# RWKV-7 scan: separate loads for r/k and v, a third buffer for the inverse's blocks, and a merge ordered behind the running sequence's first step

## The chip, the cores and the metric

The kernel runs on one core of a Trainium2 chip. The metric is the device time of one execution in microseconds (us); lower is better. A core has a matrix engine (TensorE, PE in the profile, with its weight loads as PEld), a vector engine (DVE), a scalar engine (ACT), a general engine (GpSimd, POOL) and a queue engine (SyncE, SP) which here issues nearly all the DMAs. Every engine works through its own queue in order. Engines wait for each other by semaphores.

## The reference

A decoder trunk of two layers, batch 1, 1024 tokens, width 1024. Layer 0 mixes tokens by multi-head latent attention, layer 1 by RWKV-7 time mixing; both add four heads of attention over 256 memory tokens, an output projection, a post-LayerNorm and a squared-ReLU MLP of width 4096. The change touches only the RWKV-7 mixer of layer 1, which has 12 heads of 64:

```python
p_tm = p_tm + (_token_shift(p_tm) - p_tm) * mu
r, k, v, hw, ha, hg = split(p_tm)
decay = exp(-exp(-softplus(-(w0 + tanh(hw) @ w2)) - 0.5))
a = sigmoid(a0 + ha @ a2);  g = sigmoid(hg) @ g2
kk = k * k_k / ||k * k_k||              # per head
k = k * (1 + (a - 1) * k_a)
# for every token t, per head, S is 64 x 64:
sa = S @ (-kk_t)
S = S * decay_t + sa (kk_t * a_t)^T + v_t k_t^T
y_t = S @ r_t
# group norm of y, plus (r . k . r_k) v, times g, then the output projection
```

## The kernel before, in words

The sequential recurrence is computed in chunks of 64 tokens (CH). One unit of work is two pairs of heads (u = 0, 1) times 256 tokens (QT), that is four chunks; three groups of pairs times four quarters of the sequence make 12 units, n = 0 to 11. Within a chunk the recurrence needs the inverse of a unit triangular 64 x 64 matrix per head. It is found in two stages: the 16 x 16 blocks on the diagonal by substitution on POOL, and then two merges (masks M1 and M2) that join them to blocks of 32 and 64 on PE and DVE.

A unit goes through these functions of `rwkv`:

- `prepare(n)` (L946 on) loads r, k and v in one tile `rkv` (L958) and the decay and a inputs in `sga` (L961), and finds the norm of k: squares on ACT (L967), sums on PE (L970), inverse square root on DVE, transposes and spreading on PE (L976, L982), `kk` on DVE (L986).
- `early(n)` calls `decays` for u = 0, 1 (decay products, the tiles AR, F, BK; F reads k on L1058, AR reads r on L1059, `rkk` reads r on L1069; the products of BK and AR on L1066, masked into `NR` on L1067) and then `substitute(n)`: NR is written to DRAM (L1082), the diagonal blocks read back with another layout (L1084), solved on POOL (L1085 to L1091), written to DRAM (L1093).
- `late(n)` makes what the sequence needs: masked products into `ark` (L1012, L1016), transposes `bkt` (L1020 on), `bv` (L1026, L1027, reads v) and the transposed v into `W` (L1031, reads v).
- `merge(n)` loads the solved blocks into `X` (L1101, two buffers) and does the two merges: transpose on DVE (L1106), products (L1110), mask (L1112), products (L1116), sum into X (L1117).
- `sequence(n)` is the recurrence over the four chunks. A step is: products with the state W (L1142), copy `Rs` (L1152), products with X (L1164), copy into W (L1168), products with bkt (L1172), scaled into the next W (L1175).
- `finish(n)` is the group norm and the gate, and stores o (L1208).

Iteration n of the loop writes down `sequence(n)`, `merge(n + 1)`, `prepare(n + 2)`, `early(n + 2)`, `finish(n)`, `late(n + 2)` and then `FILL[n]` pieces of other work. These pieces, 88 in all, come from one generator: 40 half projections of the layer's input (24 matmuls each, for r, k, v and the memory queries), 16 pieces of memory attention and 32 pieces of the output projection's first half (6 matmuls each). Twelve are done before the scan, `FILL[12]` at its start. Each batch of pieces is spread over the four steps of `sequence(n)` by `issue_after(anchor)`.

No queue order is written out by hand. A planner walks the program with estimated costs and puts on each engine, from what is ready in its own timeline, what was written down first. `issue_after(ins)` adds an edge: instructions of the block on the engine of `ins` are queued behind `ins`. Tiles are ring buffers of `bufs` slots; a new tile waits until all readers of the slot's last tile are done. The tiles of `ld` (rkv and sga) have two slots, which is one unit; NR has three, X two, AR, BK and rkk two (one unit).

After the loop come the rest of the pieces (`fill(99)`), the load of the output weights for o's rows 6 and 7, and the fetch of rows 4 and 5 of o. Then `out_and_ff` loads two more parts of w_out (L1816, through the raw buffers) and does the second half of the output projection.

Of the kernel before, what the change touches and what calls it, by code (L numbers as in the profile page):

```python
# [10 lines left out]
F32 = mybir.dt.float32  # L11
# [9 lines left out]
P = 128  # L21
# [5 lines left out]
NFF = 4096 // P  # L27
NM = 256
CH = 64
FILL = (4, 3, 4, 3, 4, 3, 11, 9, 7, 7, 7, 7, 7)  # L30
QT = 256
ALPHA = 4.0 ** 0.25
DECAY_C = math.exp(-0.5)
# [33 lines left out]
class Trunk:  # L67
# [588 lines left out]
    def rwkv(self, rows_src):  # L656
        nc, a, sm = self.nc, self.a, self.sm
        res_src = rows_src
        NC = QT // CH
# [5 lines left out]
        with ExitStack() as so:  # L665
# [131 lines left out]

            pieces = project()

            anchors = []  # L800

            def fill(n):
                for _ in range(n):
# [102 lines left out]
            with ExitStack() as s:  # L906
# [39 lines left out]
                def prepare(n):  # L946
                    d = DU[n] = {}
                    gr, q = n // 4, n % 4
                    d["gs"] = gs = slice(q * QT, (q + 1) * QT)
                    d["pa"] = pa = 2 * gr  # L950
                    d["ark"] = ARK[n % 2]
                    d["NR"] = up.tile([P, 2, NC, 2 * CH], F32, name="NR", bufs=3)
                    d["pC"] = up.tile([P, 2, NC], F32, name="pC", bufs=3)
                    d["AR"], d["BK"], d["rkk"] = [], [], []
                    ld, sa = [], []
                    for u in range(2):
                        t = lp.tile([P, 3, QT], F32, name="rkv")
                        nc.sync.dma_start(t, rkv_d[pa + u].rearrange("(j i) t -> i j t", i=P)[:, :, gs])  # L958
                        ld.append(t)
                        t = lp.tile([P, 2, QT], F32, name="sga")  # L960
                        nc.sync.dma_start(t, lo_d[pa + u].rearrange("(j i) t -> i j t", i=P)[:, 0:2, gs])  # L961
                        sa.append(t)

                    pk = psx.tile([P, 8], F32, name="ps_ss", tag="x")
                    for u in range(2):
                        sq = t1("sq")
                        nc.scalar.activation(sq, ld[u][:, 1, :], AF.Square, scale=self.col("kk", pa + u))  # L967
                        for t in range(2):
                            c = 4 * u + 2 * t
                            nc.tensor.matmul(pk[:, c : c + 2], sq[:, t * P : (t + 1) * P], hsel, start=True, stop=True)  # L970
                    ss = sm.tile([P, 8], F32, name="ss")
                    nc.vector.tensor_scalar(ss, pk, 1e-24, None, op0=ALU.max)
                    rs = self.rsqrt(ss, 8, "kk")
                    nc.vector.tensor_copy(cmp_[:, 0:8], rs)
                    pT = psx.tile([P, P], F32, name="ps_kT", tag="x")
                    nc.tensor.transpose(pT, cmp_, self.ident)  # L976
                    cT = tp.tile([P, P], F32, name="kT")
                    nc.scalar.copy(cT, pT)
                    pb = psx.tile([P, 2, QT], F32, name="ps_kb", tag="x")
                    for u in range(2):  # L980
                        for t in range(2):
                            nc.tensor.matmul(pb[:, u, t * P : (t + 1) * P], selk[:, 2 * u + t, :], cT, start=True, stop=True)  # L982
                    d["kk"] = []
                    for u in range(2):
                        kk = t1("kk", 2)
                        nc.vector.scalar_tensor_tensor(kk, ld[u][:, 1, :], self.col("kk", pa + u), pb[:, u, :], op0=ALU.mult, op1=ALU.mult)  # L986
                        d["kk"].append(kk)
                    d["ld"], d["sa"] = ld, sa
# [8 lines left out]

                def late(n):
                    d = DU[n]
                    ld = d["ld"]  # L1000
                    d["bv"] = up.tile([P, 2, QT], F32, name="bv")
                    d["bkt"] = up.tile([P, 2, NC, P], F32, name="bkt")
                    d["W"] = W = up.tile([P, 2, NC, 2, CH], F32, name="W")
                    if n % 4 == 0:
                        nc.gpsimd.memset(W[A, :, 0, 0, :], 0.0)
                        nc.gpsimd.memset(W[B, :, 0, 1, :], 0.0)
                    for u in range(2):
                        ark, AR, BK = d["ark"][:, u], d["AR"][u], d["BK"][u]
                        ga = psg.tile([P, NC, P], F32, name="ps_ga", tag="g")
                        for c in range(NC):  # L1010
                            for R, hd in HD:
                                nc.tensor.matmul(ga[HD[1 - hd][0], c, :], BK[R, c, 1, :], AR[R, c, :, :].rearrange("p h t -> p (h t)"), start=True, stop=True)  # L1012
                        for R, hd in HD:
                            O = HD[1 - hd][0]
                            nc.scalar.copy(ark[R, :, hd, :], AR[R].rearrange("p c h t -> p c (h t)"))
                            nc.vector.tensor_mul(ark[O, :, hd, :], ga[O], MM[O, None, :].broadcast_to([64, NC, P]))  # L1016

                        pbk = psg.tile([P, NC, P], F32, name="ps_bk", tag="g")
                        for c in range(NC):
                            nc.tensor.transpose(pbk[:, c, :], BK[:, c, :, :].rearrange("p h t -> p (h t)"), self.ident)  # L1020
                        nc.scalar.copy(d["bkt"][:, u, :, 0:64], pbk[:, :, 0:64])
                        for R, hd in HD:
                            nc.scalar.copy(d["bkt"][R, u, :, 64:P], pbk[HD[1 - hd][0], :, 64:P])

                        pbv = psx.tile([P, QT], F32, name="ps_bv", tag="x")
                        nc.tensor.matmul(pbv, blk, d["rkk"][u], start=True, stop=True)  # L1026
                        nc.vector.tensor_mul(d["bv"][:, u, :], pbv, ld[u][:, 2, :])  # L1027
                    pv = psg.tile([P, 2, 2, P], F32, name="ps_vt", tag="g")
                    for u in range(2):
                        for t in range(2):  # L1030
                            nc.tensor.transpose(pv[:, u, t, :], ld[u][:, 2, t * P : (t + 1) * P], self.ident)  # L1031
                    ev = W.rearrange("p u (w two) h i -> p u w two h i", two=2)
                    for e, R in ((0, A), (1, B)):
                        nc.scalar.copy(ev[B, :, :, e, 0, :], pv[R, :, :, 0:64])
                        nc.scalar.copy(ev[A, :, :, e, 1, :], pv[R, :, :, 64:P])
# [40 lines left out]
                def substitute(n):  # L1076
# [14 lines left out]
                    nc.gpsimd.memset(xb.rearrange("p s t -> p (s t)")[:, 0:256:17], 1.0)  # L1091
                    for h in range(8):
                        nc.sync.dma_start(blocks_of(xd, h), xb[8 * h : 8 * h + 8])  # L1093

                def merge(n):
                    d = DU[n]
                    xd = XD[n % 2]
                    N = d["NR"][:, :, :, 0:CH]
                    d["X"] = X = up.tile([P, 2, NC, CH], F32, name="X")
                    for R, hd in HD:  # L1100
                        nc.sync.dma_start(X[R].rearrange("p u c t -> p (u c t)"), rows_of(xd, hd))  # L1101
                    f2 = lambda t: t.rearrange("p c t -> p (c t)")
                    for M in (M1, M2):
                        for u in range(2):
                            XT = up.tile([P, NC, CH], F32, name="XT", bufs=1)
                            nc.vector.transpose(f2(XT), f2(X[:, u]))  # L1106
                            pq = psi.tile([P, NC, CH], F32, name="ps_q", tag="i")
                            for c in range(NC):
                                for R, hd in HD:
# [10 lines left out]
                def sequence(n):  # L1120
# [13 lines left out]
                                mm(yq[R, u, c, :], Rm[R, u, c, :], W[R, u, c, hd, :], start=False, stop=True, skip_group_check=True)  # L1134

                    anchors.clear()
                    for c in range(NC):
                        more = c < NC - 1 or nW is not None
                        qt = psq.tile([P, 2, 3, CH], F32, name="ps_q", tag="q")
# [9 lines left out]
                                    for R, hd in HD:  # L1149
                                        mm(qt[R, u, 2, :], self.ident[:, 64 * hd : 64 * hd + 64], W[:, u, c, hd, :], start=False, stop=False, skip_group_check=True)  # L1150
                        Rs = up.tile([P, 2, CH], F32, name="Rs", bufs=1)
                        nc.vector.tensor_copy(Rs, qt[:, :, 0, :])  # L1152
                        with ExitStack() as order:
                            for ins in first:
                                order.enter_context(self.tc.issue_after(ins))
# [63 lines left out]
                for n in range(N):  # L1219
                    sequence(n)  # L1220
                    if n + 1 < N:
                        merge(n + 1)
                    if n + 2 < N:
                        prepare(n + 2)
                        early(n + 2)
                    finish(n)
                    if n + 2 < N:
                        late(n + 2)
                    for c, m in enumerate(anchors):
                        with self.tc.issue_after(m):  # L1230
                            fill((FILL[n] + c) // NC)
                fill(99)
                self.wo = [self.load_split(a["w_out"][1, k * P : (k + 1) * P, :], (1024,)) for k in (6, 7)]
                for kt in (4, 5):
                    self.fetch_o(kt, kt - 2, slice(0, QT * 3))


    def out_part(self, psm, R, tt, nh, ks, wo, first):
# [684 lines left out]
```

## Time and profile before

| | |
|---|---|
| median of 3 runs | 2718.97 us (2716.73 to 2728.4) |
| profiled execution | 2722.41 us, span 2720.6 us |
| PE busy / weight loads | 2552.2 us (94%) / 2064.3 us (76%) |
| DVE busy | 1795.9 us (66%) |
| ACT busy | 1194.1 us (44%) |
| POOL busy | 212.1 us (8%) |
| mean granted PE clock | 0.965 |
| scan, 1397 to 2014 us | 617.0 us: PE busy 527.26, DVE 403.32, clock 0.90 |

The span is that of the profiled execution; its own time is a little longer, and the runs without a profile are the yardstick. In a line of the trace the first number is the start in us, the second the duration, then engine, line, operation, output<-inputs; in brackets the idle time of the engine before it and what ended that idle time. SPq is the DMA-issuing queue of SP: its duration is that of issuing. "x2" means that neighbours of one kind are merged in one row.

### The profile page before, as it was taken

The page shows a single profiled execution, that of the slowest core. Times are in us where ns is not written, and L with a number is a line of the kernel's source. Part 1 is how long each engine was busy: PE and PEld are TensorE (multiplying, and loading weights), DVE is VectorE, ACT ScalarE, POOL GpSimd, SP SyncE. Part 2 cuts the span into 40 slices and gives each one's busy share as a digit, 9 for nine tenths or more (in the row PEclk, how much of TensorE's full clock was granted, in tenths as well). Part 3 has the DMA queues.
Part 4 walks back from the last instruction along what each step waited for, and adds up shares of the span by engine and source line. Part 5 has one row for each costly group of instructions (what it writes and reads, how often), then busy time and mean ns, then how long its engine had stood idle before and what let it go on. Part 6 is the DMA issues. An engine that isn't in the chain of part 4 may idle for free. (4 is left out here: it accounts for less than half of the span.)

```text
span 2720.6 us, 41742 instructions
## 1 busy us (share of the span) xinstructions
PE 2552.2 (94%) x16189; PEld 2064.3 (76%) x16189; DVE 1795.9 (66%) x3259; ACT 1194.1 (44%) x1960; POOL 212.1 (8%) x525
## 2 busy tenths in 40 slices
PE   8999998999999999999998988878888999999998
PEld 7877776778888788877776766666667888878886
DVE  5566766487666696675355666568768766669677
ACT  4465555254444433367443333345216444443343
POOL 0012232000000000000012111111200000000000
PEclk9999999999999999999998988889999999999999
DMA  4100002235443967545532222324214444386761
GB/s 173 50 28 14 9 21 105 93 105 178 150 149 136 345 229 248 179 155 193 183 100 70 89 73 78 103 58 130 83 55 142 167 149 151 135 305 252 261 235 69
DMA packets 274581, 370.52 MB, mean 136 GB/s; under 512 B 53392, under 2 KB 152080, under 8 KB 274384
## 3 DMA queue, kind: packets, MB, share of 16 engines
q1 hardware_dynamic: 274240, 367.60, 39.6%
q8 instruction: 127, 2.08, 0.3%
q14 instruction: 70, 0.57, 0.1%
q10 hardware_dynamic: 144, 0.26, 0.0%
HBM read 258.75 MB, written 109.05 MB: 135 GB/s over the span
## 5 line engine op out<-in xcount | busy, mean ns | idle before, releaser
L143 ACT CAST Xh<-wraw 128x1024 fp32r<-128x1024 f32 (+1 forms) x138 | 139.7, 1038 | 223.5 <-PE ps_z L1643 71.0
L149 PE MATMUL ps_in<-Xh,whi 128*128 128x512 f32 x480 | 196.1, 411 | 12.0 <-ACT whi L143 8.2
L150 PE MATMUL ps_in<-Xl,whi 128*128 128x512 f32 x480 | 193.1, 402 | 0.5 <-DVE Xl L144 0.5
L151 PE MATMUL ps_in<-Xh,wlo 128*128 128x512 f32 x480 | 192.7, 402 | 0.0
L143 ACT CAST Xl<-wraw 128x1024 fp32r<-128x1024 f32 x103 | 105.1, 1050 | 154.2 <-PE ps_y L1643 48.5
L144 DVE TENSOR_TENSOR Xh<-wraw,Xh 128x1024 fp32r<-128x1024 f32 x115 | 137.9, 1220 | 52.4 <-ACT Xh L143 52.1
L144 DVE TENSOR_TENSOR Xl<-wraw,Xl 128x1024 fp32r<-128x1024 f32 x103 | 123.7, 1220 | 39.4 <-ACT Xl L143 37.2
L143 ACT CAST whi<-wraw 128x1024 fp32r<-128x1024 f32 (+3 forms) x93 | 88.3, 952 | 139.3 <-PE ps_in L150 55.1
L144 DVE TENSOR_TENSOR wlo<-wraw,whi 128x1024 fp32r<-128x1024 f32 (+3 forms) x93 | 105.3, 1135 | 65.4 <-ACT whi L143 64.9
L149 PEld LDWEIGHTS ps_in<-Xh,whi 128*128 128x128 f32 x480 | 92.6, 193 | 33.2 <-ACT whi L143 8.2
L1305 PE MATMUL ps_f<-Xh,N 128*128 128x512 f32 x320 | 106.0, 395 | 4.9 <-DVE N L144 2.2
L151 PEld LDWEIGHTS ps_in<-Xh,wlo 128*128 128x128 f32 x480 | 92.2, 192 | 19.8 <-issue 0.5
L150 PEld LDWEIGHTS ps_in<-Xl,whi 128*128 128x128 f32 x480 | 92.7, 193 | 19.1 <-DVE Xl L144 1.0
L625 ACT ACTIVATE E<-ps_s,mx,SC 128x128 f32<-128x128 f32 (+7 forms) x96 | 79.4, 831 | 50.6 <-PE ps_pt L638 24.8
L628 POOL TENSOR_TENSOR E<-E,l 128x768 f32<-128x768 f32 (+5 forms) x60 | 83.7, 1398 | 202.4 <-DVE l L626 102.2
L1305 PE MATMUL ps_f<-TB,N 128*128 128x512 f32 x384 | 92.0, 390 | 1.1 <-ACT N L143 1.1
L1643 PE MATMUL ps_y<-Xh 128*128 128x512 f32 x384 | 90.1, 389 | 0.0
L1643 PE MATMUL ps_z<-Xh 128*128 128x512 f32 x384 | 89.6, 389 | 0.0
L1643 PE MATMUL ps_z<-Xl 128*128 128x512 f32 x384 | 89.6, 389 | 0.0
L1643 PE MATMUL ps_y<-Xh,Xh 128*128 128x512 f32 x360 | 85.0, 390 | 0.0
L1305 PEld LDWEIGHTS ps_f<-TB,N 128*128 128x128 f32 x384 | 71.9, 188 | 16.5 <-ACT N L143 1.5
L1643 PEld LDWEIGHTS ps_y<-Xh 128*128 128x128 f32 x384 | 72.1, 188 | 15.0
(520 smaller groups left out, 6591.7 us busy)
## 6 DMA issues: line engine op xcount, KB each, us to landing
wraw<-in_w_ff_dram SPq DMA_DIRECT2D x182, 512.0 KB
wraw<-h_d SPq DMA_DIRECT2D x108, 512.0 KB
h_d<-slot SPq DMA_DIRECT2D x128, 256.0 KB
h_d<-tr SPq DMA_DIRECT2D x64, 256.0 KB
wraw<-in_w_in_dram SPq DMA_DIRECT2D x31, 512.0 KB
lo_d<-l_st SPq DMA_DIRECT2D x36, 256.0 KB
rkv_d<-rkv_st SPq DMA_DIRECT2D x36, 256.0 KB
rkv<-rkv_d SPq DMA_DIRECT2D x24, 384.0 KB
```

Source lines behind the costliest of these rows:

```text
L143: h = self.nc.scalar.copy(hi, src)
L144: l = self.nc.vector.tensor_sub(lo, src, f32(hi))
L149: mm(ps, wh, xh, start=first, stop=False)
L150: mm(ps, wh, xl, start=False, stop=False)
L151: mm(ps, wl, xh, start=False, stop=last)
L625: nc.scalar.activation(E3[:, g, :], S[:, g * w0 : g * w0 + n], AF.Exp, bias=mx[:, g : g + 1], scale=SC[:, i : i + 1], accum_out=l[:, g : g ...
L628: nc.gpsimd.tensor_mul(E3, E3, l[:, :, None].broadcast_to([P, nh, n]))
L1305: yield nc.tensor.matmul(ps, A[x][:, k, :], B[y][:, k, :], start=fresh and k == 0 and i == 0, stop=k == 3 and i == 2, skip_group_check=True)
L1643: m = nc.tensor.matmul(ps[t], A[x][:, u, t * P : (t + 1) * P], B[y][:, u, :], start=fresh and i == u == j == 0, stop=end and i == last_ an ...
```

## The change

Four things change. `prepare` loads r and k in a tile `rk` of two thirds of the size, and v in a tile of its own, written down behind the loads of sga; both have two slots. `substitute` now issues the load of X itself, right behind the write of the solved blocks, into one of three buffers. `merge(n + 1)` gets the first `Rs` copy of `sequence(n)` as an anchor: the transposes of the first merge (M1) are queued on DVE behind it. `FILL` is redistributed: units 0 to 10 take the 69 pieces that units 0 to 11 took, unit 11 has none, and what followed the loop (rest of the pieces, weight loads, fetches of o's first three quarters) is written down at the end of iteration 10.

```diff
-FILL = (4, 3, 4, 3, 4, 3, 11, 9, 7, 7, 7, 7, 7)
+FILL = (4, 4, 3, 4, 4, 4, 11, 9, 8, 9, 9, 0, 7)
...
-            anchors = []
+            anchors, steps = [], []
...
-                    ld, sa = [], []
+                    ld, sa, d["v"] = [], [], []
                     for u in range(2):
-                        t = lp.tile([P, 3, QT], F32, name="rkv")
-                        nc.sync.dma_start(t, rkv_d[pa + u].rearrange("(j i) t -> i j t", i=P)[:, :, gs])
+                        t = lp.tile([P, 2, QT], F32, name="rk")
+                        nc.sync.dma_start(t, rkv_d[pa + u].rearrange("(j i) t -> i j t", i=P)[:, 0:2, gs])
                         ld.append(t)
...
+                    for u in range(2):
+                        t = lp.tile([P, QT], F32, name="v")
+                        nc.sync.dma_start(t, rkv_d[pa + u, 2 * P :, gs])
+                        d["v"].append(t)
...
-                        nc.vector.tensor_mul(d["bv"][:, u, :], pbv, ld[u][:, 2, :])
+                        nc.vector.tensor_mul(d["bv"][:, u, :], pbv, d["v"][u])
...
-                            nc.tensor.transpose(pv[:, u, t, :], ld[u][:, 2, t * P : (t + 1) * P], self.ident)
+                            nc.tensor.transpose(pv[:, u, t, :], d["v"][u][:, t * P : (t + 1) * P], self.ident)
...
                     for h in range(8):
                         nc.sync.dma_start(blocks_of(xd, h), xb[8 * h : 8 * h + 8])
-
-                def merge(n):
-                    d = DU[n]
-                    xd = XD[n % 2]
-                    N = d["NR"][:, :, :, 0:CH]
-                    d["X"] = X = up.tile([P, 2, NC, CH], F32, name="X")
+                    DU[n]["X"] = X = up.tile([P, 2, NC, CH], F32, name="X", bufs=3)
                     for R, hd in HD:
                         nc.sync.dma_start(X[R].rearrange("p u c t -> p (u c t)"), rows_of(xd, hd))
+
+                def merge(n, behind=None):
+                    d = DU[n]
+                    N, X = d["NR"][:, :, :, 0:CH], d["X"]
...
-                            nc.vector.transpose(f2(XT), f2(X[:, u]))
+
+                            with self.tc.issue_after(behind) if behind is not None and M is M1 else ExitStack():
+                                nc.vector.transpose(f2(XT), f2(X[:, u]))
...
+                    steps.clear()
...
-                        nc.vector.tensor_copy(Rs, qt[:, :, 0, :])
+                        steps.append(nc.vector.tensor_copy(Rs, qt[:, :, 0, :]).ins)
...
-                        merge(n + 1)
+                        merge(n + 1, steps[0])
...
-                fill(99)
-                self.wo = [self.load_split(a["w_out"][1, k * P : (k + 1) * P, :], (1024,)) for k in (6, 7)]
-                for kt in (4, 5):
-                    self.fetch_o(kt, kt - 2, slice(0, QT * 3))
+                    if n == N - 2:
+                        fill(99)
+                        self.wo = [self.load_split(a["w_out"][1, k * P : (k + 1) * P, :], (1024,)) for k in (6, 7)]
+                        for kt in (4, 5):
+                            self.fetch_o(kt, kt - 2, slice(0, QT * 3))
```

More of the change, by code (lines that the diff above doesn't have):

```diff
@@ L999, in late @@
                     d = DU[n]
-                    ld = d["ld"]
                     d["bv"] = up.tile([P, 2, QT], F32, name="bv")
```

## The prediction

> **What bounds the kernel now.** I read the page's head and its 40 slices first, then busy time by stretches, then the queues of one unit in order of time, then the waits. The change lies in the RWKV scan only, so the first question is how much of the loss lies there.
>
> ```profile
> span 2720.6 us, 41742 instructions
> PE   8999998999999999999998988878888999999998
> PEclk9999999999999999999998988889999999999999
> ```
> A slice is 68 us. The granted clock sags in the 22nd to the 27th, PE with few exceptions in the 22nd to the 31st, from 1428 us on. The stretches put figures on it (columns: length; busy us and instruction count of PE, PEld, DVE, ACT, POOL; granted clock; DMA share; GB/s).
>
> ```profile
> 0.00:1397.00 1397.00, 1350.62 (x7078) 1096.45 (x7078) 887.70 (x1400) 675.22 (x1092) 110.07 (x146) 0.99 0.39 137
> 1397.00:2014.00 617.00, 527.26 (x6141) 414.96 (x6138) 403.32 (x1145) 215.14 (x485) 102.04 (x379) 0.90 0.28 82
> 2014.00:2720.60 706.60, 674.35 (x2976) 552.90 (x2974) 504.88 (x716) 303.76 (x386) 0.00 (x0) 0.98 0.52 183
> ```
> The twelve units' sequences run from 1397 to 2014. There PE is idle 617.00 - 527.26 = 89.7 us, and its clock is 0.90 against 0.99 before. No engine is full, so a chain of waits sets the pace. The first load of the inverse's blocks into X for unit 1 and for unit 11 give the period:
>
> ```profile
> 1441.85 0.48 SPq L1101 DMA_DIRECT2D X<-xd  x1
> ...
> 1968.11 1.14 SPq L1101 DMA_DIRECT2D X<-xd  x2
> ```
> Ten intervals in 526.3 us are 52.6 us a unit. What a unit waits for shows in its rows, here from the end of decays of unit 2 to its merge, with the start of unit 3 (put together from the queues of all engines):
>
> ```profile
> 1469.95 0.48 DVE L1069 SCALAR_TENSOR_TENSOR rkk<-rkv,vec,F 128x256 f32<-128x256 f32 x1
> 1472.89 0.69 DVE L1067 TENSOR_TENSOR NR<-ps_gn,cm 128x512 f32<-128x512 f32 x1
> 1473.61 1.23 SPq L1082 DMA_DIRECT2D nd<-NR  x2
> 1481.66 0.39 POOL L1085 COPY xb<-nb 64x256 f32<-64x256 f32 x1 [13.78 <-DMA nb<-nd]
> 1482.45 2.63 SPq L958 DMA_DIRECT2D rkv<-rkv_d  x2
> 1484.27 0.42 DVE L1027 TENSOR_TENSOR bv<-ps_bv,rkv 128x256 f32<-128x256 f32 x1 [2.71 <-PE ps_bv L1026]
> 1485.47 0.51 ACT L967 ACTIVATE sq<-rkv,vec 128x256 f32<-128x256 f32 x1 [1.29 <-DMA rkv<-rkv_d]
> 1492.92 2.86 SPq L1093 DMA_DIRECT2D xd<-xb  x8
> 1495.67 0.45 PE L1164 MATMUL ps_q<-Rs,X 64*64 64x64 f32 x8
> 1495.94 0.49 SPq L1101 DMA_DIRECT2D X<-xd  x1
> 1501.31 0.45 DVE L1106 STREAM_TRANSPOSE XT<-X 128x256 f32<-128x256 f32 x1 [5.92 <-DMA X<-xd]
> 1501.81 1.12 PE L1110 MATMUL ps_q<-XT,NR 64*64 64x64 f32 x16 [3.66 <-DVE rsq_t L164]
> 1501.92 0.58 DVE L1168 COPY W<-ps_q 64x128 f32<-64x128 f32 x2
> 1523.63 1.23 SPq L1082 DMA_DIRECT2D nd<-NR  x2
> ```
> Two things are to be seen. First, a loop: r and k of unit 2 are read for the last time at 1470.4, v in the same tile only at 1484.7, and unit 3's loads go out between these v reads, at 1482.45 and after. From there the way is load, square, norm, decays, NR (1523.6), substitution, X, merge. NR to NR is 1523.6 - 1473.6 = 50 us, and some 14 us of it (1470.4 to 1484.7) wait for v alone. Second, DVE takes its queue in order: it stands 5.92 us at XT until X lands, while the running sequence's own copy L1168, whose matmul was through at 1496.12, sits behind it till 1501.92, and PE runs dry for 3.66 us.
>
> **The change, part by part.**
>
> *r and k apart from v.* Unit n+2's r and k wait for decays(n+1) instead of late(n+1). Shift in the unit above: 14.3 us. The last scan unit gives nearly the same, 1893.93 + 0.47 to 1909.50 + 0.43, 15.5 us:
>
> ```profile
> 1893.93 0.47 DVE L1069 SCALAR_TENSOR_TENSOR rkk<-rkv,vec,F 128x256 f32<-128x256 f32 x1
> ...
> 1909.50 0.43 DVE L1027 TENSOR_TENSOR bv<-ps_bv,rkv 128x256 f32<-128x256 f32 x1
> ```
> This does not come off the period whole: the decays of n+2 write AR, BK and rkk, which late(n+1) still reads, and the list of PE work is unchanged. What it can take is idle time that these readers end. In the scan the waits are (us in all, times, longest):
>
> ```profile
> PE ps_ss L970 <- ACT sq L967: 17.0, 6, 4.1
> DVE F L1058 <- DMA rkv<-rkv_d: 41.3, 9, 9.8
> DVE XT L1106 <- DMA X<-xd: 35.6, 10, 7.0
> L1110 PE MATMUL ps_q<-XT,NR 64*64 64x64 f32 x768 | 40.4, 247 | 20.7 <-DVE XT L1106 8.4 <-DVE rsq_t L165 5.0 <-DVE rsq_y L166 3.7
> ```
> PE loses 17.0 us waiting for squares of a k that is late. I book all of it. Bounds: 0 if the order of work moves the squares forward with the load, and 14.3 x 10 = 143 us if the loop alone set the pace, which PE's idle of 89.7 cuts off first.
>
> *Third X buffer, X loaded with the substitution, merge behind the first step.* The X load already goes out right behind the xd write (1492.92 + 2.86 = 1495.78 against 1495.94), so moving the line by itself gains nothing; SP would wait there for the same 2.86 us burst. The third buffer lets X(n+2) land while X(n) is still read and X(n+1) waits: with r and k earlier the substitution can run one sequence ahead, and the merge then meets an X that is there. I book the idle in front of the merge's first matmul, 20.7 us, bounds 0 (X still just in time) and that plus the rest of the 35.6 us for which DVE stood. The added edge costs nothing as things stand: the Rs copies of the sequence in question are
>
> ```profile
> 1464.15 0.28 DVE L1152 COPY Rs<-ps_q 128x128 f32<-128x128 f32 x1
> 1481.28 0.28 DVE L1152 COPY Rs<-ps_q 128x128 f32<-128x128 f32 x1
> 1491.26 0.29 DVE L1152 COPY Rs<-ps_q 128x128 f32<-128x128 f32 x1
> ```
> and M1's first transpose at 1501.31 comes after the third, so an edge to the first does not bind. Behind a held merge stand only its own later pieces; if the edge bound, the merge would still start three steps before its user.
>
> *DMAs.* Each unit has two more issues on SP, v apart. An issue is about 0.49 us by the X row, 24 of them 11.8 us of SP, with one new wait, for v's own slot; v's readers come in late(n+2), far behind the norm, and hide it. I book 0. The bytes stay the same.
>
> ```profile
> rkv<-rkv_d SPq DMA_DIRECT2D x24, 384.0 KB
> ```
> The load above went from issue to reader in 1485.47 - 1482.45 = 3.0 us for 384 KB; at 256 KB it is no longer. The Trainium skill (DMA: Bandwidth & Descriptors, Anatomy of one DMA — SWDGE (gpsimd) path) says each DMA pays about 2.0 us whatever its size, on the POOL-fed path, which speaks against splitting: 24 x 2.0 = 48 us as an estimate if they ran one after another on the path, which the 3.0 us row neither shows nor excludes for this queue.
>
> *FILL and the end.* Units 0 to 10 now take all 69 pieces that units 0 to 11 took, so seven output pieces leave the last unit. A piece is six matmuls; at 0.46 us (the longest of the three groups' means) it is 2.8 us, seven 19 us.
>
> ```profile
> L149 PE MATMUL ps_o<-whi,Xh 128*128 128x512 f32 x66 | 30.2, 461 | 2.9 <-DVE Xl L1247 1.7 <-DVE Xh L1247 0.9 <-DVE Xh L1245 0.2
> 2016.74 0.39 PE L151 MATMUL ps_o<-whi,Xl 128*128 128x512 f32 x1
> ...
> 2019.35 2.30 SPq L1816 DMA_DIRECT2D wraw<-in_w_out_dram  x2
> ...
> 2023.99 0.79 PE L149 MATMUL ps_o<-slot,Xh 128*128 128x512 f32 x1 [6.85 <-ACT slot L143]
> ```
> They move into units that have 89.7 us idle, and leave a last sequence that the output rows can fill; booked 0, bounds 19 either way. The early loads of w_out and of o free the raw buffers that L1816 waited for, so the 6.85 us hole at its end goes: 6.85 (bounds 0 and 6.85).
>
> Sum: 17.0 + 20.7 + 6.85 = 44.6 us. The profiled execution took 2722.4 us (span 2720.6), so 2677.8; the runs' median is 2718.97, 3.4 lower, so I predict 2675.
>
> **Rivals.**
>
> *A, no change (2712).* The planner's list keeps merge(n+1) ahead of decays(n+2) on DVE and PE, the early data wait in SBUF, and the stalls keep their size. For it: F and XT are placed before their data land now (41.3 and 35.6 us), so the placement, not only the slot, is at fault. Against it: unit 3's squares ran as soon as its load landed. Only the end gains: 2718.97 - 6.85 = 2712.
>
> *B, slower (2745).* DVE's queue is the place: reads of r and k are put still further ahead of their landing, and the sequence's copies stand behind them. Today a wait at F is 41.3 / 9 = 4.6 us; at the longest seen, 9.8, in ten units it costs 98 - 41.3 = 57 us more, less 6.85, so 2769 at worst; half of it is 2745 with the gains gone. It decides once this wait exceeds 4.1 + 44.6 / 10 = 8.6 us a unit. For it: DVE runs in order and already holds the sequence up. Against it: the load is smaller and its slot free long before.
>
> *C, the clock comes back too (2632).* The clock is low only where PE has gaps:
>
> ```profile
> 1260.00:1280.00 20.00, 20.00 (x90) 16.57 (x89) 9.09 (x13) 16.25 (x27) 1.03 (x7) 1.00 0.44 158
> 1500.00:1520.00 20.00, 17.49 (x222) 14.72 (x223) 13.77 (x42) 5.34 (x13) 0.23 (x3) 0.74 0.17 58
> ```
> If the scan's clock rose from 0.90 to the 0.98 of the stage behind it, its 527.26 us of PE work would shrink by 527.26 x (1 - 0.90 / 0.98) = 43 us, on top of the 44.6: 2632. For it: full slices run at 1.00. Against it: many of these matmuls are 64 columns wide and paced by their waits. The Trainium skill (TensorE: Matmul & The Clock Gate, Part 1) says that the clock is halved after an idle window of about 3.4 us; by that rule removing 3.66 us gaps must give clock back. The trace agrees in kind: 0.74 over 20 us is 10.4 us at half speed, in a slice with such a gap.
>
> **How the numbers follow.** Forecast (2650 to 2705) 0.46, C 0.20, A 0.19, B 0.15. The range leaves out the lower half of C and the worse half of B: 2632 to 2745; the likeliest case alone has 2650 to 2705. Half a per cent, 13.6 us, is about what a measurement of this kernel tells from none: faster than 2705.4 is the forecast and C, 0.66, same is A, 0.19, slower is B, 0.15.
>
> **What would show it.** Right: r/k loads go out within 2 us of the previous unit's last rkk, not after bv; waits at XT fall below 10 us in all and M1's transposes come in the first or second step; X-to-X is 48 to 49 us; PE idle in the scan is below 60 us; no hole of 6 us ahead of the first output row. Wrong: the period stays at 52 us with NR still behind the merge (A), DVE's wait at the first reader of r or k grows past 8.6 us a unit (B), or the scan's clock passes 0.95 (C).

## The result, and the profile after

The kernel after takes 2679.23 us (median of 4 runs, 2673.1 to 2683.53), the kernel before 2717.85 us beside it (4 runs, 2715.32 to 2728.4). The ratio is 0.9849, with a 95% interval of 0.9815 to 0.9883: faster by 1.2 to 1.9%. The profiled execution took 2682.22 us, 40.2 less than the 2722.41 before. The prediction was 2675, so the number came out. Most of the steps that it was added up from did not, as the experiments show.

The head of the page of the kernel after:

```profile
span 2680.4 us, 41837 instructions
...
PE   8999999999999999999998989888988999999998
...
PEclk9999999999999999999998989899989999999999
```

The clock still sags in the 22nd, 24th, 26th and 30th slice, in four slices where before it was five. The stretches put figures on it. They are cut where the last y of the scan is copied out (the ACT row L1182 below); in the kernel before that copy starts at 2013.91. Columns as in the prediction: length; busy us and count of PE, PEld, DVE, ACT, POOL; granted clock; DMA share; GB/s.

```profile
1397.00:1986.60 589.60, 513.35 (x6145) 400.62 (x6143) 406.67 (x1135) 215.81 (x487) 108.81 (x381) 0.92 0.30 89
1986.60:2680.40 693.80, 666.60 (x2956) 548.07 (x2956) 496.52 (x710) 299.86 (x381) 0.00 (x0) 0.98 0.52 184
```

The copy of the last y in the kernel after, from ACT's queue:

```profile
1986.61 0.58 ACT L1182 COPY yd<-ps_y 128x512 f32<-128x512 f32 x1 [3.08 <-PE ps_y L1138]
```

The same cut of the kernel before:

```profile
1397.00:2013.90 616.90, 527.16 (x6141) 414.96 (x6138) 403.22 (x1145) 215.04 (x484) 102.04 (x379) 0.90 0.28 82
2013.90:2720.60 706.70, 674.45 (x2976) 552.90 (x2974) 504.98 (x716) 303.86 (x386) 0.00 (x0) 0.98 0.52 183
```

The scan is 27.3 us shorter and the rest 12.9 us. PE's busy time in the rest falls by 674.45 - 666.60 = 7.9 us with 20 matmuls fewer: work that now runs inside the scan. Inside the scan PE's idle time falls from 616.90 - 527.16 = 89.7 to 589.60 - 513.35 = 76.3 us, 13.4 less, and PE's busy time by 13.8 us with nearly the same number of matmuls, at a clock of 0.92 in place of 0.90.

Waits of the scan after (us in all, times, longest):

```profile
DVE XT L1110 <- DMA X<-xd: 31.9, 9, 7.4
DVE W L1180 <- PE ps_q L1177: 28.4, 12, 4.8
ACT sq L971 <- PE ps_ss L974: 23.6, 7, 10.6
ACT sq L971 <- DMA rk<-rkv_d: 7.0, 4, 2.8
```

Two of PE's groups there (behind the first bar busy time and mean ns of one, behind the second the idle time before them and what ended it):

```profile
L1114 PE MATMUL ps_q<-XT,NR 64*64 64x64 f32 x768 | 36.7, 232 | 19.2 <-DVE XT L1110 8.2 <-DVE cmpk L978 6.9 <-DVE ss L976 2.6
L974 PE MATMUL ps_ss<-hsel,sq 128*128 128x2 f32 x80 | 12.1, 256 | 1.4 <-DVE bv L1030 1.4
```

PE's wait for the squares (17.0 us before) is gone from its row, and DVE's wait at F for r and k (41.3 us) is no longer among the waits; ACT's wait for the load of r and k falls from 57.8 to 7.0 us. The wait of DVE for X at the merge's transposes stays: 31.9 us against 35.6. The idle time before the merge's first matmul stays too: 19.2 against 20.7. In its place before the squares stands something new: ACT waits 23.6 us for PE's ps_ss, the sums of the squares, not for a load.

Unit 3, from the queues of all engines (lines of the kernel after; L958 is the load of r and k, L971 the squares, L974 their sums, L990 kk, L1030 bv, L1072 rkk):

```profile
1432.72 1.36 SPq L958 DMA_DIRECT2D rk<-rkv_d  x1
1468.96 0.29 DVE L1157 COPY Rs<-ps_q 128x128 f32<-128x128 f32 x1 [0.87 <-PE ps_q L1155]
1469.17 0.44 DVE L1110 STREAM_TRANSPOSE XT<-X 128x256 f32<-128x256 f32 x1
1483.76 0.39 DVE L1030 TENSOR_TENSOR bv<-ps_bv,v 128x256 f32<-128x256 f32 x1
1488.86 0.61 PE L974 MATMUL ps_ss<-hsel,sq 128*128 128x2 f32 x4
1489.50 0.51 ACT L971 ACTIVATE sq<-rk,vec 128x256 f32<-128x256 f32 x1 [10.62 <-PE ps_ss L974]
1507.65 0.87 DVE L990 SCALAR_TENSOR_TENSOR kk<-rk,vec,ps_kb 128x256 f32<-128x256 f32 x2 [0.19 <-PE ps_kb L986]
1508.16 0.37 SPq L958 DMA_DIRECT2D rk<-rkv_d  x1
1516.04 0.47 DVE L1072 SCALAR_TENSOR_TENSOR rkk<-rk,vec,F 128x256 f32<-128x256 f32 x1
1516.54 0.36 SPq L958 DMA_DIRECT2D rk<-rkv_d  x1
1519.78 0.55 SPq L1085 DMA_DIRECT2D nd<-NR  x1
1546.05 0.45 DVE L1110 STREAM_TRANSPOSE XT<-X 128x256 f32<-128x256 f32 x1 [6.15 <-DMA X<-xd]
```

Two things are to be seen. Loads of r and k, here those of unit 4, now go out when the last reader of r and k is done (1508.16 behind kk, 1516.54 behind rkk that ends at 1516.51), no longer between the reads of v. But r and k of unit 3, requested by 1432.72, had their first sums on PE at 1488.86, 56 us later, and 5 us behind the last bv of unit 2 at 1483.76. So the early data lay in SBUF. NR goes out only at 1519.78, and the merge meets X 6.15 us late at 1546.05, as before.

At the end the hole of 6.85 us ahead of the first output row is gone; some of the rows that stood behind it run beside the last steps of the sequence (L1138 belongs to it):

```profile
1984.89 1.05 PE L149 MATMUL ps_o<-slot,Xh 128*128 128x512 f32 x2
1985.87 0.69 PE L1138 MATMUL ps_y<-W,NR 64*64 64x64 f32 x8
1986.50 0.79 PE L150 MATMUL ps_o<-slot,Xh 128*128 128x512 f32 x1
```

### The profile page after: what moved, and what is told of

Its sections match the earlier page's. It is cut to its first block, busy times and chain, and to the rows that moved or that the text cites. A ratio compares the mean times of both kernels' runs of the same rounds, so it can differ in the third digit from the quotient of the medians.

```text
span 2680.4 us, 41837 instructions
## 1 busy us (share of the span) xinstructions
PE 2531.7 (94%) x16189; PEld 2046.3 (76%) x16189; DVE 1793.9 (67%) x3259; ACT 1191.1 (44%) x1960; POOL 217.5 (8%) x525
## 5 line engine op out<-in xcount | busy, mean ns | idle before, releaser
L625 ACT ACTIVATE E<-ps_s,mx,SC 128x128 f32<-128x128 f32 (+7 forms) x96 | 79.4, 831 | 51.3 <-PE ps_pt L638 24.9
```

The source lines that it names most:

```text
L625: nc.scalar.activation(E3[:, g, :], S[:, g * w0 : g * w0 + n], AF.Exp, bias=mx[:, g : g + 1], scale=SC[:, i : i + 1], accum_out=l[:, g : g ...
```

## The experiments

The first theories were three: L, the slot loop over v that the prediction put first; T, the moved pieces and the moved end; X, the third buffer. Later came S (the stalls belong to buffers and to the end) against N (every rewriting draws a new plan, and the plan before is a bad draw), and P (the pieces of units 0 to 5) against E (the end). All times are medians, all ratios are to runs of the kernel before on the same chip, and the runs were made on several chips; "scan end" is the start of the last y copy in the profiled execution.

| kernel | time us | ratio, 95% | scan end | PE idle in scan | clock |
|---|---|---|---|---|---|
| before | 2717.85 | | 2013.91 | 89.7 | 0.90 |
| after | 2679.23 | 0.9849 [0.9815, 0.9883] | 1986.61 | 76.3 | 0.92 |
| split of r, k and v alone | 2679.5 | 0.9857 [0.9832, 0.9882] | 1977.09 | 77.8 | 0.93 |
| third X buffer alone | 2719.97 | 0.9999 [0.9989, 1.0008] | 2017.89 | 92.5 | 0.89 |
| new FILL and end alone | 2672.34 | 0.9823 [0.9795, 0.985] | 1979.34 | 75.7 | 0.94 |
| after without the split | 2675.64 | 0.9839 [0.9816, 0.9862] | 1975.48 | 71.3 | 0.94 |
| split and third buffer | 2685.73 | 0.9883 [0.9865, 0.9901] | 1979.35 | 78.8 | 0.93 |
| split, buffer, edge | 2667.52 | 0.9813 [0.9787, 0.9839] | 1958.48 | 59.7 | 0.94 |
| split, buffer, edge, end | 2665.49 | 0.9798 [0.9783, 0.9812] | 1964.71 | 59.3 | 0.93 |
| pieces of units 0 to 5 alone | 2683.05 | 0.9878 [0.9854, 0.9902] | 1970.31 | 75.1 | 0.95 |
| end alone | 2716.6 | 0.9991 [0.9978, 1.0003] | 2011.87 | 87.5 | 0.90 |
| sga loads first | 2721.3 | 1.0004 [0.9995, 1.0014] | 2012.99 | 89.1 | 0.90 |
| one piece moved late | 2722.17 | 1.0003 [0.9989, 1.0018] | 2013.29 | 86.7 | 0.89 |
| split, buffer, edge, end, two banks | 2664.35 | 0.9801 [0.9779, 0.9822] | 1976.00 | 57.6 | 0.92 |

Idle time is the length of the stretch from 1397 to the scan's end less PE's busy time in it.

**The split alone.** The kernel before with r and k loaded apart from v, and nothing else.

```diff
-                        t = lp.tile([P, 3, QT], F32, name="rkv")
+                        t = lp.tile([P, 2, QT], F32, name="rk")
...
+                        t = lp.tile([P, QT], F32, name="v")
```

> Before, with r and k loaded apart from v and nothing else (two X buffers, X loaded in the merge, old FILL and old end). Theory L (v's slot holds the loop of loads and decays): r and k come some 14 us earlier, PE's 17 us of waiting for the squares goes, while X can still not run a sequence ahead; 2718 - 17 = about 2700, and the scan ends 10 to 17 us earlier than 2014 us. Rival T (the gain is the moved output pieces and the early loads at the end): 2718 with a scan that ends at 2014 us.

It ran at 2679.5 us: this part by itself is worth as much as the whole change. Its scan:

```profile
1397.00:1977.10 580.10, 502.26 (x6135) 396.11 (x6134) 402.92 (x1130) 214.45 (x485) 104.65 (x381) 0.93 0.30 88
```

and PE's group of the sums in it:

```profile
L974 PE MATMUL ps_ss<-hsel,sq 128*128 128x2 f32 x80 | 11.5, 248 | 0.6 <-DVE bv L1030 0.4
```

PE's wait for squares is gone, idle time falls by 11.9 us and busy time by 24.9 us. So two thirds of the scan's gain of 36.8 us come as a shorter busy time at a higher clock, which the forecast's sum had not booked. Both theories missed: L said 2700, T 2718.

**The third X buffer alone.** Kernel before with X loaded in the substitution into one of three buffers, without the edge.

```diff
+                    DU[n]["X"] = X = up.tile([P, 2, NC, CH], F32, name="X", bufs=3)
+                    for R, hd in HD:
+                        nc.sync.dma_start(X[R].rearrange("p u c t -> p (u c t)"), rows_of(xd, hd))
...
-                    d["X"] = X = up.tile([P, 2, NC, CH], F32, name="X")
-                    for R, hd in HD:
-                        nc.sync.dma_start(X[R].rearrange("p u c t -> p (u c t)"), rows_of(xd, hd))
```

> Before, with three X buffers and X loaded in the substitution, no edge, rkv joint, old FILL. With the new FILL this part and the edge together moved the scan's end by 4 us (1979.3 to 1975.5). Theory S: the same here, 2714 to 2718. Rival N: 2680 to 2700.

2719.97 us, no change within 0.1%. Theory X falls: a third slot of X by itself brings nothing.

**FILL and the end alone.** Kernel before with the change's FILL and the code behind the loop moved into iteration 10.

```diff
-FILL = (4, 3, 4, 3, 4, 3, 11, 9, 7, 7, 7, 7, 7)
+FILL = (4, 4, 3, 4, 4, 4, 11, 9, 8, 9, 9, 0, 7)
...
+                    if n == N - 2:
+                        fill(99)
```

> Before, with only the new FILL and the rest of the pieces, the output weights and the fetches of o written down at the end of iteration 10. Theory L: the hole of 6.85 us ahead of the output rows goes and the last sequence runs bare, 2718 - 7 to - 13 = 2705 to 2711. Rival T: nearly the whole gain, about 2685.

2672.34 us, also as much as the whole, without the split. The scan alone is 34.6 us shorter, although the wait of squares for the load is still there at 41.6 us (57.8 before). So neither L nor T holds alone (for this run L said 2705 to 2711, T 2685): each part by itself brings some 40 us or more, and both together bring no more than one.

**After without the split.**

```diff
-                        t = lp.tile([P, 2, QT], F32, name="rk")
+                        t = lp.tile([P, 3, QT], F32, name="rkv")
```

> After, with r, k and v again in one tile and one load (third X buffer, edge, FILL and end kept). Theory L: the scan falls back by most of its gain of 27 us, so 2679 + 20 to 27 = about 2702. Rival T: 2679 stays. Rival X (the third buffer alone opens the way): 2679 to 2685.

2675.64 us, and its interval overlaps that of the kernel after. On top of the new FILL the split, the buffer and the edge bring nothing that can be measured.

**After with the old FILL and the old end** (the split, the third buffer and the edge).

```diff
-FILL = (4, 4, 3, 4, 4, 4, 11, 9, 8, 9, 9, 0, 7)
+FILL = (4, 3, 4, 3, 4, 3, 11, 9, 7, 7, 7, 7, 7)
```

> After, with the old FILL and the old end after the loop. Theory L: the part behind the scan falls back by its gain of 13 us, 2692. Rival T: most of the gain goes, 2710 or more.

2667.52 us, where both theories had it slower than the whole. With 59.7 us the scan has 16.6 us less idle time than the kernel after, though the intervals of the two times still overlap. The next run asks whether the old pieces are the better ones once the split is in.

**The same with the new end.** FILL = (4, 3, 4, 3, 4, 3, 11, 9, 9, 9, 10, 0, 7): the old pieces in units 0 to 5, and the end of the change.

> After, with the old FILL for units 0 to 7 and 9, 9, 10, 0 for the last four, so that the first units have no more pieces than before while the end is the new one. Theory S: the gains of split and buffer with the old FILL (scan end 1958) and of the new end (13 us) add up: 2667 - 13 = 2654. Rival N: 2660 to 2690, anywhere.

2665.49 us, 0.9798 [0.9783, 0.9812]. It beats both kernels; against the after's 0.9849 [0.9815, 0.9883] the intervals just part. The 2654 that Theory S added up did not come: the end, moved on top of the rest, brings no gain that the intervals show. The stage behind the scan is 2663.4 - 1964.7 = 698.7 us long.

**Two edits that should do nothing.** The sga loads written down ahead of those of rkv; and one piece moved from unit 11 to unit 10.

```diff
-FILL = (4, 3, 4, 3, 4, 3, 11, 9, 7, 7, 7, 7, 7)
+FILL = (4, 3, 4, 3, 4, 3, 11, 9, 7, 7, 8, 6, 7)
```

> Before, with the two loads of a head pair written down in the other order (sga ahead of rkv). The same instructions, the same waits; only the order in which the planner meets two loads changes. Theory S (before has stalls that belong to its buffers and its end, which the parts of the change remove): 2718 within half a per cent, the scan ends at 2014 us within 8. Rival N (the planner's list is sensitive, and before is a bad draw, which any small change leaves): 2680 to 2700.

> Before, with one output piece moved from unit 11 to unit 10, FILL (.., 7, 7, 8, 6, 7). Theory S: 2716 to 2718 (a piece is under 3 us). Rival N: 2680 to 2700, and then the scan's units differ from the first one on where the order differs.

2721.3 and 2722.17 us, ratios 1.0004 and 1.0003. Theory N falls in this form: these rewritings, and the third buffer, left the time where it was. A piece late in the scan may move; whether an early one may is what the next two runs ask.

**The end alone, and the early pieces alone.**

The first line belongs to the end alone, which also has the code behind the loop moved, the second to the early pieces alone with the old end.

```diff
+FILL = (4, 3, 4, 3, 4, 3, 11, 9, 9, 9, 10, 0, 7)
...
+FILL = (4, 4, 3, 4, 4, 4, 11, 9, 7, 7, 5, 7, 7)
```

> The kernel before with the code behind the loop moved to the end of iteration 10, and the pieces of units 8 to 11 moved with it (9, 9, 10, 0); units 0 to 5 keep their old pieces. Theory P (the pieces of units 0 to 5 are what took 35 us off the scan in the run with FILL and the end alone): the scan still ends within 5 us of 2013.9, only the rest behind it is 13 us shorter, time 2702 to 2712. Theory E (moving the end or the pieces of the last units is enough): the scan ends 20 us or more earlier, time under 2690.

> The kernel before with the pieces of units 0 to 5 as in the change (4, 4, 3, 4, 4, 4), paid for in unit 10 (5 in place of 7, unit 8 and 9 stay 7), the end where it was. Theory P: the scan ends near 1979, the rest stays 707, time 2682 to 2692. Theory E: the time stays at 2715 to 2722. If half comes from each, about 2702.

P holds: the end alone gives 2716.6 us, not told apart from no change, with 702.5 us behind the scan against 706.7; the early pieces alone give 2683.05. New entries for units 0 to 5, 23 pieces in place of 21 with the two taken from unit 10, shorten the scan by 43.6 us:

```profile
1397.00:1970.30 573.30, 498.23 (x6133) 390.58 (x6131) 401.14 (x1144) 214.30 (x483) 107.66 (x379) 0.95 0.30 88
```

with these waits for the loads, and PE's group of the sums:

```profile
ACT sq L967 <- DMA rkv<-rkv_d: 39.0, 13, 6.8
DVE F L1058 <- DMA rkv<-rkv_d: 17.1, 9, 3.8
L970 PE MATMUL ps_ss<-hsel,sq 128*128 128x2 f32 x84 | 12.3, 251 | 5.0 <-ACT sq L967 3.2 <-ACT pr L695 1.8
```

A batch of pieces is spread over the four steps of a sequence: at step c, counted from 0, (FILL + c) // 4 are taken, so an entry of 3 gives none at the first step and an entry of 4 gives one. The two waits above were 57.8 and 41.3 us before and shrink the most; PE's own wait for the squares falls from 17.0 to 3.2 us, the wait that the split removes. That the extra piece fills the gap left by the load is argued from these rows, not isolated.

**The buffer without the edge, on top of the split** (old FILL and old end).

```diff
-                        merge(n + 1, steps[0])
+                        merge(n + 1)
```

> Split and third X buffer with the load in the substitution, without the edge on the merge's transposes, old FILL and old end. The split alone ran at 2679.5, the split with buffer and edge at 2667.5. If the edge is what gives the 12 us between them: 2677 to 2682. If the buffer and the earlier load give them: 2665 to 2670, and the edge is worth nothing. The waits for X at the transposes should stay near 31 us in either case, since the load of X waits for POOL's solved blocks and not for a slot.

2685.73 us, 0.9883 [0.9865, 0.9901]: the buffer adds nothing to the split (0.9857 [0.9832, 0.9882]), and with the edge the kernel is 18 us faster (0.9813 [0.9787, 0.9839]). The scan without the edge, its stretch and the group of the merge's first matmul:

```profile
1397.00:1979.40 582.40, 503.57 (x6143) 397.35 (x6141) 402.49 (x1130) 214.51 (x485) 105.53 (x381) 0.93 0.30 88
```

```profile
L1112 PE MATMUL ps_q<-XT,NR 64*64 64x64 f32 x768 | 38.1, 235 | 22.5 <-DVE XT L1108 15.2 <-DVE rsq_t L165 4.0 <-DVE cmpk L978 3.2
```

The same two with it:

```profile
1397.00:1958.50 561.50, 501.76 (x6129) 395.55 (x6127) 402.45 (x1130) 213.96 (x485) 108.91 (x381) 0.94 0.31 91
```

```profile
L1113 PE MATMUL ps_q<-XT,NR 64*64 64x64 f32 x768 | 36.2, 229 | 14.3 <-DVE rsq_t L164 7.0 <-DVE XT L1109 6.8 <-DVE vr L1198 0.5
```

The edge takes 78.8 - 59.7 = 19.1 us of idle time and next to no busy time; 8.2 of it stand in the row of the merge's first matmul. The kernel with the edge is 15 us ahead at unit 7's y copy, the two stand level again at unit 8's (1837.57 and 1837.08), and 15.7 us of the difference lie in the interval of unit 9, 67.8 us without the edge and 52.1 with it. The only place where the edge was seen to bind is the merge of unit 2, whose first transpose stands at 1464.78 without it and at 1469.61, directly behind the Rs copy of 1469.40, with it. How a hold of 5 us there leads to another order of work eight units later stays open. Nor is it shown that holding the merge is what helps: this is one new order of work against one other, and a rewriting that should do nothing was tried only on the kernel before, not on the kernels with the split.

**Two PSUM banks for the norm.** The products of the norm (ps_ss, ps_kT, ps_kb), of bv (ps_bv) and of the group norm (ps_yo) share one bank, taken in turn in the order in which they are written down. The run gives them two and the merges one, on top of the fastest version.

```diff
-                psi = pool(s, "psi", 2, space=PSUM)
+                psi = pool(s, "psi", 1, space=PSUM)
...
-                psx = pool(s, "psx", 1, space=PSUM)
+                psx = pool(s, "psx", 2, space=PSUM)
```

> The kernel after with the old pieces in units 0 to 5 (this ran at 2665.5), and one PSUM bank taken from the merges (2 to 1) and given to the norm and decay products (1 to 2). If the single bank of these products is the next limit in the period of a unit (kk waited 11 us behind cmpk in unit 3): 2645 to 2660. If the bank is not the limit, or the merges need both of theirs: 2665 or more, up to 2690.

2664.35 us: no gain over 2665.49. So either this bank does not set the time, or the bank that the merges gave up costs what it brings; this run can't tell. But it shows the order in which the norm takes its turn, in one unit's rows:

```profile
1740.25 0.42 DVE L1030 TENSOR_TENSOR bv<-ps_bv,v 128x256 f32<-128x256 f32 x1
1740.73 0.61 PE L974 MATMUL ps_ss<-hsel,sq 128*128 128x2 f32 x4 [0.44 <-DVE bv L1030]
1741.18 0.41 DVE L1030 TENSOR_TENSOR bv<-ps_bv,v 128x256 f32<-128x256 f32 x1
```

With two banks the first sums of a unit come ahead of the second bv of the unit before in six of ten units; with one bank they never did, in any unit of the 13 other kernels. The two ps_bv are the last tiles written down in this ring ahead of the next unit's ps_ss. With one slot ps_ss takes over from the second of them, with two from the first, which is what the rows show.

## Why the prediction was right and where it was wrong

The time was right, 2675 against 2679, by steps of which some brought far more than booked and some nothing. By profiled executions 40.2 us came off where 44.6 were booked. That the errors of the steps nearly cancel is luck.

**r and k apart from v, 17.0 us booked.** The mechanism was right, and the sign for it was met: PE's wait for squares went from 17.0 us to none in its row, and 20 of the 22 loads go out within 0.1 us of the last reader of r and k. The size of this term was off in two ways. The gain alone is 41.9 us by medians, because the sum booked idle time only, and 24.9 of the 36.8 us of the scan came as busy time at a clock of 0.93 in place of 0.90. And the shift of 14.3 us a unit did not reach the norm, because of an order that the prediction did not look at: the turns in the one PSUM bank. Unit 7 shows it. Before, with loads, squares and sums behind the last bv:

```profile
1704.49 0.42 DVE L1027 TENSOR_TENSOR bv<-ps_bv,rkv 128x256 f32<-128x256 f32 x1 [2.79 <-PE ps_bv L1026]
1714.19 0.54 SPq L958 DMA_DIRECT2D rkv<-rkv_d  x1
1717.75 0.51 ACT L967 ACTIVATE sq<-rkv,vec 128x256 f32<-128x256 f32 x1 [10.26 <-DMA rkv<-rkv_d]
1718.32 0.78 PE L970 MATMUL ps_ss<-hsel,sq 128*128 128x2 f32 x4 [3.86 <-ACT sq L967]
```

After, with the read of ps_yo ahead of bv:

```profile
1665.54 0.37 SPq L958 DMA_DIRECT2D rk<-rkv_d  x1
1671.52 0.36 SPq L958 DMA_DIRECT2D rk<-rkv_d  x1
1683.35 1.02 ACT L1210 ACTIVATE o<-ps_yo,vec 128x256 f32<-128x256 f32 x2 [3.08 <-PE ps_yo L1207]
1689.22 0.42 DVE L1030 TENSOR_TENSOR bv<-ps_bv,v 128x256 f32<-128x256 f32 x1 [1.41 <-PE ps_bv L1029]
1693.29 0.50 PE L974 MATMUL ps_ss<-hsel,sq 128*128 128x2 f32 x4
```

The load went from 9.7 us behind the last bv to 23.7 us ahead of it, but the sums only from 13.8 us behind it to 4.1 us behind it. Over ten units the first sums stand 6.3 us behind the last bv before and 1.8 us after: this link of the loop lost 4.4 us a unit, not 14.3, and with one bank it has no more than the 1.8 left to lose. By the same measure the split alone has 1.6 us, the kernels with early pieces and a joint load 4.4 to 4.6, and the kernels that stayed at 2717 to 2722 have 6.3 to 6.9. The bv is only the last link. Ahead of it in the same ring stands ps_yo, the group norm of a sequence that has ended, so with one bank the sums of unit n + 3 must wait until ps_yo of unit n is read. They came 7.6 us behind that read in the mean of the kernel after and 12.9 us in the kernel before, and never ahead of it in any of the 14 kernels. This ties the norm to the end of a sequence, however early r and k arrive. No run takes ps_yo out of the ring, so what that would gain is not known. The Trainium skill (Perfetto Trace Analysis, Identifying Performance Opportunities, Optimization Strategy) says that a gap which repeats over a stretch can mean that there is no PSUM for the next tile; the order of the rows with one and with two banks agrees in kind, but the idle time of the scan, 59.3 us with one bank and 57.6 with two, does not show that this shortage sets the time.

**Third X buffer, early X load and merge, 20.7 us booked.** Of this idle time only 1.5 us came off (20.7 to 19.2). The step that failed is "with r and k earlier the substitution can run one sequence ahead": r and k were earlier, the norm was not, so from unit 3 on X still landed when DVE was already waiting for it, or just before, and the waits at XT are 31.9 us against a sign of under 10. The other signs of this step fell with it: PE's idle time in the scan is 76.3 us and not below 60, M1's transposes moved to the first step for unit 2 (1469.17) but not for unit 3 (1546.05, behind the third Rs copy of its sequence at 1534.79), and the loads of X, of unit 1 and of unit 11, stand (1940.89 - 1432.14) / 10 = 50.9 us apart from unit to unit, not 48 to 49:

```profile
1432.14 0.48 SPq L1099 DMA_DIRECT2D X<-xd  x1
...
1940.89 1.58 SPq L1099 DMA_DIRECT2D X<-xd  x2
```

Moving the X load's line gained nothing, as stated: 2719.97 us by itself.

**The edge, booked as costing nothing because it does not bind.** Wrong in the other direction. It binds once, and on top of the split and the old FILL the kernel with it is 18 us faster, by a way that stays open. The prediction judged it by the order of before, where M1's transposes stood behind the third Rs copy; with the split the merge of unit 2 runs ahead of the first (1464.78 against 1472.45 without the edge).

**The moved end, 6.85 us booked.** The hole is gone and what follows the scan is 12.9 us shorter in the kernel after. By itself on the kernel before the move shortened it by 4.2 us, within the bounds of 0 and 6.85, since a hole was left there:

```profile
2015.52 0.79 PE L149 MATMUL ps_o<-slot,Xh 128*128 128x512 f32 x1 [3.69 <-ACT slot L143]
```

In the kernel after part of the second half of the output runs ahead of the scan's end, so 7.9 of the 12.9 us are work that moved into the scan.

**FILL, booked 0 within 19 us either way.** The largest miss. The step that failed is that it priced seven output pieces leaving the last unit, and did not price the entries of units 0 to 5 at all. These alone give 38 us, twice the bound. On top of the split they do the opposite: with the split, buffer, edge and end in both, the new early entries make 2679.23 of 2665.49. Both remedies cut the same wait, that of PE for the squares (17.0 us before, none with the split, 3.2 with the early pieces), and are not to be added. The bound itself was too wide: it took 0.46 us as the price of a matmul, but in the kernel after back-to-back matmuls of the output start 0.23 us apart (1992.56, 1992.79, 1993.02), which makes seven pieces about 10 us, by this estimate. Why the second costs some 14 us once the first is in, and does not just do nothing, the runs do not settle; the scan's idle time is 76.3 us with the new entries and 59.3 with the old.

**DMAs, booked 0.** Right: the kernel after and its variant without the split, with 24 issues fewer, are not told apart. An issue of v takes 0.32 to 0.59 us on SP in the kernel after. A reader that waits for r and k stands 2.7 us behind their issue at 256 KB (1422.77 to 1425.44 in unit 3 of the kernel after) and 3.0 us at 384 KB, so most of this time does not go with the size. That agrees in kind with the fixed 2 us a DMA of the Trainium skill (DMA: Bandwidth & Descriptors, Anatomy of one DMA — SWDGE (gpsimd) path), which is stated there for another path; that 24 of them add up to 48 us is not what the runs show.

**The rivals.** A named the right mechanism for the X part, early data that wait in SBUF, but put the cause in the planner's list. B is out: DVE's waits at r and k went away. C came in part. The clock went to 0.92 after, 0.95 at most among these kernels, not to 0.98, but the busy time that came with it is the larger part of what the split alone gained.

**How it came to fit.** Put in one after the other, by medians and across batches, the parts read: split 2679.5, buffer 2685.7 (no difference by the intervals), edge 2667.5, end 2665.5, early entries 2679.2. The split gave 25 us more than booked, the buffer at least 20.7 less, the edge 18 more, the end 5 less, and the early entries 14 less. The sum fits because these errors have both signs; none of its three terms was right in size by these runs.

## What to carry to other kernels

Before a gain is booked from an earlier load, follow its first consumer to every ring that it takes a slot from, PSUM banks too: the tiles that are written down ahead in that ring, here those of bv and of the group norm, are predecessors that the flow of data does not show. Where two edits cure the same wait, expect the larger of the two and not their sum, and run each alone and each left out: here the change with its early entries of the table taken back ran 0.5% faster than the whole. Filler work has a price by place: here two more pieces in the first six units moved the time by 38 us one way and, on top of the split, by 14 us the other.

## What the runs showed of the hardware

The scan's time is PE's idle time plus its busy time, and the busy time depends on the granted clock: busy time times clock is nearly constant, 527.16 x 0.90 = 474 us before, 513.35 x 0.92 = 472 after, 502.26 x 0.93 = 467 with the split alone, 498.23 x 0.95 = 473 with the early pieces alone. So a stall can cost more than its length: with the split alone 11.9 us less idle time came with 24.9 us less busy time. It is no fixed factor, for the edge took 19.1 us of idle time and brought only 1.8 of busy time, and the two banks have 57.6 us of idle time at a clock of 0.92.

What decides it can be read from narrow stretches, here of the kernel before around the wait of unit 2's merge:

```profile
1496.75:1500.16 3.41, 1.40 (x7) 0.80 (x5) 0.00 (x0) 1.31 (x2) 0.37 (x2) 1.00 0.78 228
1500.16:1503.57 3.41, 1.74 (x24) 1.44 (x24) 2.01 (x11) 0.00 (x0) 0.00 (x0) 0.50 0.24 80
1503.57:1506.99 3.42, 2.73 (x35) 2.42 (x36) 3.22 (x10) 0.27 (x1) 0.00 (x0) 0.50 0.02 5
1506.99:1510.40 3.41, 3.41 (x32) 2.73 (x33) 0.73 (x3) 0.00 (x0) 0.00 (x0) 0.50 0.20 77
1510.40:1513.81 3.41, 3.41 (x57) 3.08 (x58) 2.41 (x7) 0.00 (x0) 0.00 (x0) 1.00 0.00 0
```

The clock is either 1.00 or 0.50 and changes on a grid of 3.41 us. PE is busy for 1.40 of the 3.41 us of one window, and the next three windows run at half clock, though PE is busy through the third of them. In the scan of the kernel before such stretches at half clock add up to 122.9 us, in the kernel after to 91.2, with the split alone to 78.5, with the early pieces alone to 58.0. Taken over the scans of all 14 kernels, 157 of the 159 windows at full clock in which PE was busy less than half of the time were followed by one at half clock, and 3 of the 1711 in which it was busy 70% or more. So idle time that comes in one piece, or that gathers in one window, also costs clock, and idle time spread thin does not: the two banks have 88.7 us at half clock for 57.6 us of idle time, the kernel with split, buffer and edge 68.3 for 59.7.

The Trainium skill (TensorE: Matmul & The Clock Gate, Part 1) has the clock either full or halved, switched by the activity in windows of about 3.4 us. The rows agree; but where the Trainium skill asks for an idle window before the clock is halved, a window in which PE was busy for 41% was enough here.
